# Decayed cumulative sum after a matmul: own gate tiles for the warm-up, the decay squares written by ScalarE, and a new order for the first 32 slots

## The chip, the core and the metric

The kernel runs on one NeuronCore of a Trainium2 chip. The core has five engines that run their own instruction queues in order: TensorE (PE; its weight loads are listed apart as PEld), VectorE (DVE), ScalarE (ACT), GpSimd (POOL) and SyncE (SP, which only issues DMAs here). The metric is the device time of one execution in microseconds (us). Before the change the median of four runs is 908.17 us.

## The reference, cut to what matters

```python
B, S, D = 16, 2048, 1024
# x: (B, S, D) f32, w: (D, D) f32, decay: (D,) f32 in 0.05 .. 0.95
xw = x @ w
out[:, 0, :] = xw[:, 0, :]
for t in range(1, S):
    out[:, t, :] = decay[None, :] * out[:, t - 1, :] + xw[:, t, :]
```

For each batch and each output column the product `x @ w` runs through a first-order recurrence along time, with one decay per column.

## The kernel before

**Tiling.** The 16 x 2048 rows are cut into 64 chunks of 512 time steps (`TL`), four for each batch. Two neighbouring chunks form a group. One group and one set `n` of 128 output columns (there are K = 8) form a *slot*, which is one tile of 128 columns by 1024 time steps; only the last group has one chunk. A slot needs 16 matmuls: 8 blocks of the contraction (k) for each of the two chunks, each 128x128 weights against 128x512 of x, summed in PSUM.

**Input.** POOL loads x as bf16 into `xb` (`load`, line 101; 3 buffers), a quarter (32 partitions) per DMA. VectorE turns it in 32x32 blocks into `xw` (`turn`, line 110; 2 buffers), two bf16 at a time, and a copy takes the even and odd rows apart into `xt` (`part`, line 119; 5 buffers), which is what TensorE reads. Part m of `xt` serves k = 2m and 2m + 1. The weights come in by DMA in four pieces (halves of the columns h, even or odd rows e) and are copied to `wsb` (`settle`, line 295); sixteen such copies are numbered 0 to 15, by h, e and m.

**The recurrence** has two ways. An unpaired tile is scanned by VectorE straight from PSUM (`scan`, L216, over 1024 steps). A paired tile is first folded: ScalarE copies PSUM to `xs` (`copy`, L178) and scales the odd columns by the decay (`odd`, L164), POOL adds the two (`join`, L191), VectorE scans half the steps with the squared decay (L196), then ScalarE scales the result (`even`, L164) and POOL fills in the other half (`fill`, L241). Pairing takes work from VectorE and gives it to ScalarE and POOL. Each fourth tile is unpaired, and the slots named in `flips` are the other way round. `save` keeps the last column for the next group of the same batch (L245); `zero` writes the column before the first step (POOL memset, or ScalarE copy of the kept column, L187).

**Output.** VectorE turns the scanned tile back (`back`, L253); after four tiles SP stores them in four DMAs (L274).

**The order of the work** is written out by hand. All instructions are pinned to the order in which the program emits them, so each engine works through its own part of that order. At each slot the matmuls are emitted, then the deeds that `agenda` lists for that slot; from slot 34 on a rule (`usual`) makes the list, and the last 20 slots have their own. A deed is a letter and a number:

- M, U: loads of halves of chunks 0 and 1, of weight pieces; L: the next x load of a list
- W, w: one weight copy, by VectorE or by ScalarE
- K: a warm-up copy and its spins; D: the decay and its squares; d: the squares once more, into PSUM (`square_again`, line 350)
- E, F, G: quarter turns of chunks 0 and 1, and their copies by VectorE (F) and ScalarE (G)
- T: a whole turn of a chunk; t, u: its first and second half; X, Y: the copies of its two halves by ScalarE
- p, g, z, j: copy, odd, zero, join; S: scan; h, c, k: even, fill, save; B: back

**The start.** While the first loads are under way, TensorE multiplies zeros (`spin`, line 309) so that its clock is up when data comes: 22 matmuls, then for each quarter q of chunk 0 a copy of one column of x into `idle` (`spin_on`, line 327) and three more matmuls that read `idle`. Slots 0 to 3 are computed together at slot 0, in the order in which pieces of chunks 0 and 1 come in: 32 matmuls of 256 columns (even k of chunk 0), 16 of 512 (odd k), then 64 of 256 (chunk 1). They go to three PSUM buffers `ps` and, for tile 3, to `spare` and `spare1`. Slots 4 to 7 take even k first. Slots 8 and 9 are computed together: chunk 2 for both, then chunk 3 for both. Slot s from 4 on takes one of the three `ps` buffers in turn, and waits until the tile before in it has been read.

Of the kernel before, what the change touches and what calls it, by code (L numbers as in the profile page):

```python
# [10 lines left out]
BF16 = mybir.dt.bfloat16  # L11
# [3 lines left out]
def _ap(ap_obj: bass.AP, new_ap, extra_offset=0):  # L15
    return dataclasses.replace(
        ap_obj,
        ap=[list(p) for p in new_ap],
        offset=ap_obj.offset + extra_offset,
    )  # L20
# [5 lines left out]
def kernel(  # L26
# [26 lines left out]
    nc = tc.nc  # L53
    pin = tc.keep_in_program_order
    B, S, D = x.shape
    assert w.shape == (D, D)

    NQ = 4
    P = 32
    CQ = D // NQ  # L60
    K = CQ // P
    M = K // 2
    TL = 512
    NJ = TL // P
# [5 lines left out]
    const = ctx.enter_context(tc.tile_pool(name="const", bufs=1))  # L70
# [5 lines left out]
    def ring(pool, name, count, shape, dtype=FP32):  # L76
        i = turns[name] = turns.get(name, -1) + 1
        return pool.tile(shape, dtype, name=f"{name}{i % count}")

    def quad(q):  # L80
        return slice(q * P, (q + 1) * P)
# [8 lines left out]
    squares = [const.tile([128, K], FP32, name="squares")]  # L90
# [6 lines left out]
    xb_of = {}  # L97
# [12 lines left out]
    def turn(c, j0=0, j1=NJ, m0=0, m1=M):  # L110
        if c not in xw_of:
            xw_of[c] = ring(sb, "xw", 2, [128, M, NJ, P, 2], BF16)
        src = xb_of[c][:, j0:j1].rearrange("p j c -> p (j c)").bitcast(FP32)
        dst = xw_of[c].rearrange("p m j i e -> p (m j i e)").bitcast(FP32)
        pin(nc.vector.transpose(  # L115
            out=dst.rearrange("p (m j i) -> p j m i", m=M, i=P)[:, j0:j1, m0:m1],
            in_=src.rearrange("p (j m c) -> p j m c", m=M, c=P)[:, :, m0:m1]))

    def part(c, copy, m0, m1, j0=0, j1=NJ):
        if c not in xt_of:  # L120
            xt_of[c] = ring(sb, "xt", 5, [128, M, 2, TL], BF16)
        src = xw_of[c][:, m0:m1, j0:j1].rearrange("p m j i e -> p m e (j i)")
        pin(copy(out=xt_of[c][:, m0:m1, :, j0 * P:j1 * P], in_=src))  # L123
# [176 lines left out]
    idle = const.tile([128, TL], BF16, name="idle")  # L300
    spare = ring(psp, "spare", 1, [128, TL])
# [4 lines left out]
    pin(nc.vector.memset(rows, 0.0))  # L306
    pin(nc.scalar.copy(out=touch, in_=idle[:, 0:1]))

    def spin(count):
        for _ in range(count):  # L310
            pin(nc.tensor.matmul(  # L311
                out=spare, lhsT=idle[:, 0:128], rhs=idle, start=True, stop=True))

    spin(22)
    H = NJ // 2
    halves = ((0, H), (H, NJ))
    for q in range(NQ):
        pin(nc.sync.dma_start(
            out=rows[q * P:q * P + R],
            in_=_ap(decay, [[P, R], [CH, 2], [1, P]], q * CR)))  # L320
# [4 lines left out]
            load(i // 2, q, *halves[i % 2])  # L325

    def spin_on(q):
        pin(nc.scalar.copy(out=idle[quad(q), 0:1], in_=xb_of[0][quad(q), 0, 0:1]))  # L328
        spin(3)

    def load_part(i):
        load_w((nc.gpsimd,), *((0, 1), (1, 0), (1, 1))[i])
# [13 lines left out]
    def square(i):  # L346
        pin(nc.vector.tensor_tensor(
            out=squares[-1][:, 0:K], in0=dec, in1=dec, op=ALU.mult))

    def square_again(i):  # L350
        squares.append(ring(psp, "spare1", 1, [128, TL]))
        square(0)


    ident = const.tile([128, 128], FP32, name="ident")
# [37 lines left out]
    slots += [([c], n) for c in groups[-1] for n in range(K)]  # L393
    tiles = []

    def turn_half(half):
        def act(c):
            if half == 0:
                turn(c, 0, NJ, 0, 2)
            else:  # L400
                turn_and_load(c, 2)
        return act

    def turn_and_load(c, m0=0):
        turn(c, 0, NJ, m0, M)
        if 2 <= c < nch - 3:
            loads.extend((c + 3, q) for q in range(NQ))

# [4 lines left out]
        "C": lambda s: tiles[s % len(slots)].complete(),  # L413
        "B": lambda s: tiles[s % len(slots)].back(),
        "T": turn_and_load,
        "t": turn_half(0),
        "u": turn_half(1),
        "X": lambda c: part(c, nc.scalar.copy, 0, 2),
        "Y": lambda c: part(c, nc.scalar.copy, 2, M),
        "x": lambda c: part(c, nc.vector.tensor_copy, 0, 2),  # L420
# [6 lines left out]
        "F": lambda i: part_one(i, nc.vector.tensor_copy),  # L427
        "G": lambda i: part_one(i, nc.scalar.copy),
        "K": spin_on,
        "D": decays,  # L430
        "d": square_again,
        "I": identity,
        "V": ending,
# [9 lines left out]
        "L": lambda i: load(*loads.pop(0)) if loads else None,  # L443
    }
    agenda = {
        -99: "M0 M1 U0 M2 M3 U1 U2 D W0 w1 W2 w3 K0 K1 K2 K3 E0 F0 G1 E1 F2 G3 E2 F4 G5 E3 F6 G7 W4 w5 W6 w7 E4 F8 G9 E5 F10 G11 E6 F12 G13 E7 F14 G15 L L L",
        0: "W8 w10 W9 W11",
        1: "S0 L",
        2: "L p1 z1",
        3: "L p2 z2 L B0 g1 L w15 W12 j1 S3 k0 w14 w13 L g2",  # L450
        4: "L d k3 j2 B3 p4 S1 L g4 z4 L",
        5: "t2 h1 j4 k1 S2 X2 c1 S4 k2 h2",
        6: "B1 k4 h4 c2 p5 u2 c4 g5 t3 p6 j5 B4",
        7: "g6 Y2 L u3 L z5 j6 B2 X3 S5 L z6 L Y3 S6 L L S7 k6 k5 L h5 h6 c5 T4",
        8: "p8",
        9: "c6 k7 g8",
        10: "p9 L g9 B7 j8 X4 B6 L j9",
        11: "B5 z8 p10 L g10 S8 z9 z10 j10 z11 Y4 S9",
        12: "L S10 h8 h9 c8 T5 h10 c9 p11 B8",
        13: "g11 c10 p12 B9 X5 L L B10 j11 Y5",  # L460
        14: "T6 L z12 g12 j12 S13 z14 X6",
        15: "L p14 S11 L g14 B13 h11 j14 Y6",
        16: "S12 c11 S14 h12 L p15 B11 c12 g15",
        17: "T7 L z15 p16 j15 g16 h14 L S15 X7 c14 B12",
        18: "j16 h15 B14 p17 L g17 z16 z17 c15 S16 Y7",
        19: "j17 B15 h16 L S17 k16 p18 z18 L T8 c16 h17",
        20: "k17 g18 c17 p19 B16 X8 j18 B17 L",
        21: "g19 S18 L Y8 z19 j19 S20 L h18 k18 c18",
        22: "p21 S19 z21 k20 g21 L T9 h19 j21 k19 c19",
        23: "B20 p22 L g22 B18 j22 B19 z22 L",  # L470
        24: "S21 p23 z23 X9 S22 h21",
        25: "k21 S24 g23 c21 k22 Y9 j23 B21 h22",
        26: "c22 S23 z25 p25 g25 B24 h23 j25 B22 k23 c23",
        27: "T10 z26 p26 g26 j26 B23 X10 S25",
        28: "Y10 S27 z28 h25 S26 c25",
        29: "p28 B27 g28 h26 j28 B25 c26 S28 z29",
        30: "p29 T11 g29 h28 j29 B26 c28",
        31: "p30 S29 z30 g30 B28 j30 h29 c29 S30",
        32: "S31 B29 h30 c30 p32 g32 z32 j32 B30 B31 L L",
        33: "p33 g33 z33 j33 S32 h32 c32 k32 L L",  # L480
        -20: "z-20",
# [17 lines left out]
        -2: "S-3 S-4",  # L499
        -1: "S-2 h-4 c-4 a-1 b-1 V",  # L500
    }
    flips = (0, 11, 13, 15, 19, 20, 23, 24, -19, -18, -16, -11, -8, -6, -3, -2)
    later = {}
    begun = {"T": 12, "X": 11, "Y": 11}
    for c in range(5, nch):
# [127 lines left out]
```

## Time and profile before

| What | Value |
|---|---|
| median of 4 runs | 908.17 us (908.13 to 908.73) |
| profiled execution | 908.43 us, span 906.6 us |
| granted TensorE clock | 0.999 of full speed |
| busy share: TensorE, VectorE, ScalarE, POOL | 99%, 91%, 76%, 73% |
| VectorE busy from 32 to 62 us | 100% |
| ScalarE busy from 42 to 52 us | 10.0 of 10 us |
| VectorE's waits on x, whole run | 6.1 us in 5 waits, longest 2.5 |
| DMA traffic | 204.77 MB, mean 226 GB/s |

A timeline row gives the start, the busy time, the engine, the line, the operation, its output and inputs, shapes, and a count; in brackets stands how long the engine was idle before it and what ended that wait. A row of the waits gives who waited for whom, then the total in us, the number of waits and the longest. Matmuls overlap by their pipeline, so their pace is read from start to start.

### The profile page before, as it was taken

To read this page: it belongs to the slowest core of one execution; us is meant where nothing else is said; L and a number is where in the kernel's file an instruction comes from. 1 tells how busy PE (TensorE), PEld (TensorE's weight loads), DVE (VectorE), ACT (ScalarE), POOL (GpSimd) and SP (SyncE) were. 2 spreads that over 40 slices of the span, in tenths; PEclk is the share of its full clock that TensorE was granted. 3 is DMA by queue.
4 is the path that set the end of the run, shared out by engine and by line. 5 is a ranking of instruction groups with operands and counts; after the bars stand their busy time and mean duration, and the time that the engine had idled before them with its cause. 6 is when DMAs were issued, how large, how long until landed. Compare 5 with 4: busy or idle time off the path is not lost.

```text
span 906.6 us, 11980 instructions
## 1 busy us (share of the span) xinstructions
PE 893.3 (99%) x4120; PEld 411.4 (45%) x4202; DVE 827.9 (91%) x622; ACT 684.9 (76%) x950; POOL 657.8 (73%) x756
## 2 busy tenths in 40 slices
PE   8999999999999999999999999999999999999997
PEld 4444444444444444444444444444444444444444
DVE  4989998999999999999999999999999999999997
ACT  4799867877877778778778778777787787787742
POOL 7888768778777777777677786777777776776622
PEclk9999999999999999999999999999999999999999
DMA  9999999999999999999999999999999999999868
GB/s 193 166 211 215 217 253 213 215 235 252 255 252 239 248 251 246 251 242 230 223 235 226 224 231 224 236 229 224 232 232 225 228 233 222 227 231 213 176 146 233
DMA packets 402542, 204.77 MB, mean 226 GB/s; under 512 B 8752, under 2 KB 401456, under 8 KB 402480
## 3 DMA queue, kind: packets, MB, share of 16 engines
q1 hardware_dynamic: 265168, 134.76, 60.9%
q0 software_dynamic: 137024, 68.70, 56.5%
q8 instruction: 33, 0.54, 0.2%
q10 hardware_dynamic: 288, 0.52, 0.2%
q14 instruction: 29, 0.24, 0.1%
HBM read 138.42 MB, written 134.22 MB: 301 GB/s over the span
## 4 chain that ended last, share of the span: by engine, by line
PE 95%; ACT 2%; DVE 2%; issue 1%; POOL 0%; DVEq 0%; ACTq 0%
PE ps L126 92%; PE spare L311 1%; DVE so L216 1%; PE spare L126 1%; ACT xs L178 1%; ACT h L164 1%; ACT xt L123 0%; DVE ot L253 0%; DVE so L196 0%; ACT wsb L297 0%; POOL xs L191 0%; PE spare L375 0%; PE ps L375 0%; ACT idle L328 0%; ACT keep L245 0%
## 5 line engine op out<-in xcount | busy, mean ns | idle before, releaser
L126 PE MATMUL ps<-xt,wsb 128*128 128x512 bf16 (+1 forms) x4010 | 873.6, 377 | 6.0 <-ACT xt L123 1.4
L126 PEld LDWEIGHTS <-wsb 128*128 128x128 bf16 x4152 | 406.1, 98 | 480.5 <-issue 2.1
L191 POOL TENSOR_TENSOR xs<-h,xs 128x512 f32<-128x512 f32 (+1 forms) x190 | 243.3, 1281 | 193.9 <-ACT h L164 94.0
L178 ACT COPY xs<-ps 128x1024 f32<-128x1024 f32 (+1 forms) x190 | 189.8, 999 | 156.8 <-PE ps L126 146.2
L253 DVE STREAM_TRANSPOSE ot<-so 128x1024 f32<-128x1024 f32 (+1 forms) x260 | 300.1, 1191 | 1.3 <-POOL so L241 0.4
L241 POOL TENSOR_TENSOR so<-h,xs 128x512 f32<-128x512 f32 (+1 forms) x190 | 241.9, 1274 | 41.0 <-ACT h L164 20.3
L123 ACT COPY xt<-xw 128x2048 bf16<-128x2048 bf16 (+1 forms) x132 | 240.3, 1825 | 7.4 <-DVE xw L115 7.3
L105 POOL DMA_DIRECT2D xb<-in_x_dram x264 | 173.9, 660 | 2.7 <-DMA ot<-in_w_dram 1.3
L164 ACT ACTIVATE h<-so,dec 128x512 f32<-128x512 f32 (+1 forms) x190 | 145.2, 766 | 23.8 <-DVE so L196 20.3
L115 DVE STREAM_TRANSPOSE xw<-xb 128x2048 f32<-128x2048 f32 (+2 forms) x72 | 147.5, 2050 | 6.1 <-DMA xb<-in_x_dram 6.1
L196 DVE TENSOR_TENSOR_SCAN so<-spare,keep,xs 128x512 f32<-128x512 f32 (+1 forms) x96 | 119.3, 1245 | 27.6 <-POOL xs L191 27.3
L196 DVE TENSOR_TENSOR_SCAN so<-spare,xs 128x512 f32<-128x512 f32 x94 | 114.4, 1219 | 28.5 <-POOL xs L191 25.8
L164 ACT ACTIVATE h<-ps,dec 128x512 f32<-128x512 f32 (+1 forms) x190 | 130.5, 687 | 0.0
L216 DVE TENSOR_TENSOR_SCAN so<-dec,keep,ps 128x1024 f32<-128x1024 f32 (+1 forms) x36 | 77.1, 2143 | 0.1
L216 DVE TENSOR_TENSOR_SCAN so<-dec,ps 128x1024 f32<-128x1024 f32 x33 | 74.6, 2261 | 1.8 <-PE ps L126 1.2
L245 ACT COPY keep<-so 128x1 f32<-128x1 f32 x136 | 25.5, 188 | 12.8 <-DVE so L216 12.8
L187 ACT COPY so<-keep 128x1 f32<-128x1 f32 x96 | 18.2, 192 | 5.2 <-DVE ot L253 5.2
L311 PE MATMUL spare<-idle 128*128 128x512 bf16 x34 | 10.8, 474 | 2.4 <-DVE idle L305 1.2
L126 PE MATMUL spare<-xt,wsb 128*128 128x256 bf16 (+1 forms) x60 | 12.6, 322 | 0.0
L185 POOL MEMSET so<- 128x1 f32 x94 | 10.9, 116 | 0.6 <-DVE ot L253 0.6
L290 POOL DMA_DIRECT2D ot<-in_w_dram x12 | 6.7, 560 | 3.2 <-DMA xb<-in_x_dram 1.9
L311 PEld LDWEIGHTS <-idle 128*128 128x128 bf16 x34 | 3.6, 117 | 9.2 <-issue 3.5
(32 smaller groups left out, 30.5 us busy)
## 6 DMA issues: line engine op xcount, KB each, us to landing
out_dram<-ot SPq DMA_DIRECT2D x248, 512.0 KB, 10.9
xb<-in_x_dram POOLq DMA_DIRECT2D x248, 256.0 KB, 7.9
out_dram<-ot SPq DMA_DIRECT2D x12, 256.0 KB, 4.3
xb<-in_x_dram POOLq DMA_DIRECT2D x16, 128.0 KB, 5.7
ot<-in_w_dram POOLq DMA_DIRECT2D x12, 128.0 KB, 5.1
out_dram<-xb SPq DMA_DIRECT2D x3, 256.0 KB
ot<-in_w_dram ACTq DMA_DIRECT2D x2, 256.0 KB, 5.1
ot<-in_w_dram SPq DMA_DIRECT2D x2, 256.0 KB, 4.7
```

Of the source, the lines that this page charges most:

```text
L105: pin(nc.gpsimd.dma_start(out=xb_of[c][quad(q), j0:j1], in_=_ap(x, [[D, P], [P * D, j1 - j0], [1, CQ]], (b * S + t0 + j0 * P) * D + q * CQ)))
L115: pin(nc.vector.transpose(out=dst.rearrange("p (m j i) -> p j m i", m=M, i=P)[:, j0:j1, m0:m1], in_=src.rearrange("p (j m c) -> p j m c", ...
L123: pin(copy(out=xt_of[c][:, m0:m1, :, j0 * P:j1 * P], in_=src))
L126: pin(nc.tensor.matmul(out=ps[:, t0:t1] if ps.shape[1] >= t1 else ps, lhsT=wsb[:, k, n].rearrange("p q i -> p (q i)"), rhs=xt[:, k // 2, k ...
L164: pin(nc.scalar.activation(out=h, in_=src, func=mybir.ActivationFunctionType.Copy, scale=dec[:, self.n:self.n + 1]))
L178: pin(nc.scalar.copy(out=self.xs, in_=self.ps))
L191: pin(nc.gpsimd.tensor_tensor(out=odds, in0=self.g, in1=odds, op=ALU.add))
L196: pin(nc.vector.tensor_tensor_scan(out=so[:, 3:T + 2:2], data0=squares[-1][:, n:n + 1].to_broadcast([128, T // 2]), data1=self.xs[:, 1:T:2 ...
L216: pin(nc.vector.tensor_tensor_scan(out=so[:, t + 2:t + 2 + size], data0=dec[:, n:n + 1].to_broadcast([128, size]), data1=ps, initial=befor ...
L241: pin(nc.gpsimd.tensor_tensor(out=self.so[:, 2:T + 2:2], in0=self.h, in1=self.xs[:, 0:T:2], op=ALU.add))
L245: pin(nc.scalar.copy(out=self.keep, in_=self.so[:, self.T + 1:self.T + 2]))
L253: pin(nc.vector.transpose(out=outlet.ot[:, :, c0:c0 + P], in_=self.so[:, 2 + t0:2 + t0 + nj * P].rearrange("p (i t) -> p i t", t=P)))
```

## The change

Four things change. (1) Each of the four warm-up groups has its own 128x128 tile `gate`, zeroed by VectorE before the first spin; the copy from x goes to that tile, and the group's spins use it as weights. The last group spins twice instead of three times. (2) The second squaring into PSUM (`d`) is a ScalarE copy of the squares made before, where it was a VectorE multiplication. (3) The agenda of the head and of slots 0 to 31 is reordered, D comes after G3 instead of before W0, and which engine does some weight copies changes. In `flips`, 1 and 12 come in and 13 and 15 go: tiles 1, 12 and 15 become unpaired, tile 13 paired. (4) Chunks 2 and 3 are turned whole (T) instead of in halves (t, u).

```diff
+    gates = [const.tile([128, 128], BF16, name=f"gate{q}") for q in range(NQ)]
+    for gate in gates:
+        pin(nc.vector.memset(gate, 0.0))
+
+    def spin(count, by):
         for _ in range(count):
-            pin(nc.tensor.matmul(
-                out=spare, lhsT=idle[:, 0:128], rhs=idle, start=True, stop=True))
-    spin(22)
+            pin(nc.tensor.matmul(out=spare, lhsT=by, rhs=idle, start=True, stop=True))
+    spin(22, idle[:, 0:128])
...
     def spin_on(q):
-        pin(nc.scalar.copy(out=idle[quad(q), 0:1], in_=xb_of[0][quad(q), 0, 0:1]))
-        spin(3)
+        pin(nc.scalar.copy(out=gates[q][quad(q), 0:1], in_=xb_of[0][quad(q), 0, 0:1]))
+        spin(3 if q < NQ - 1 else 2, gates[q])
...
     def square_again(i):
         squares.append(ring(psp, "spare1", 1, [128, TL]))
-        square(0)
+        pin(nc.scalar.copy(out=squares[1][:, 0:K], in_=squares[0]))
...
-        -99: "M0 M1 U0 M2 M3 U1 U2 D W0 w1 W2 w3 K0 K1 K2 K3 E0 F0 G1 E1 F2 G3 E2 F4 G5 E3 F6 G7 W4 w5 W6 w7 E4 F8 G9 E5 F10 G11 E6 F12 G13 E7 F14 G15 L L L",
-        0: "W8 w10 W9 W11",
+        -99: "M0 M1 U0 M2 M3 U1 U2 W0 w1 W2 w3 K0 K1 K2 K3 E0 F0 G1 E1 F2 G3 D E2 F4 G5 E3 F6 G7 W4 w5 W6 w7 E4 F8 G9 E5 F10 G11 E6 F12 G13 E7 F14 G15 L L L",
+        0: "W8 w11 W9 W10",
         1: "S0 L",
-        2: "L p1 z1",
-        3: "L p2 z2 L B0 g1 L w15 W12 j1 S3 k0 w14 w13 L g2",
-        4: "L d k3 j2 B3 p4 S1 L g4 z4 L",
-        5: "t2 h1 j4 k1 S2 X2 c1 S4 k2 h2",
-        6: "B1 k4 h4 c2 p5 u2 c4 g5 t3 p6 j5 B4",
-        7: "g6 Y2 L u3 L z5 j6 B2 X3 S5 L z6 L Y3 S6 L L S7 k6 k5 L h5 h6 c5 T4",
+        2: "L",
+        3: "L p2 L S1 g2 z2 L w14 j2 w12 w13 S3 k0 L w15",
+        4: "k1 L",
+        5: "p4 B0 L d g4 S2 z4 k3 j4 T2 h2 L",
+        6: "k2 p5 c2 g5 S4 L X2 j5 B1",
+        7: "Y2 L B2 L L T3 p6 z5 z6 g6 k4 h4 j6 B3 X3 L S5 L Y3 S6 L L S7 c4 h6 k6 h5 c6 B4",
         8: "p8",
-        9: "c6 k7 g8",
-        10: "p9 L g9 B7 j8 X4 B6 L j9",
-        11: "B5 z8 p10 L g10 S8 z9 z10 j10 z11 Y4 S9",
-        12: "L S10 h8 h9 c8 T5 h10 c9 p11 B8",
+        9: "c5 g8 B7",
+        10: "k7 k5 z8 j8 p9 B5 g9 S8 j9 z9 T4",
+        11: "h8 p10 c8 g10 S9 X4 L j10 B8",
+        12: "p11 L B6 L Y4 T5 L z10 z11",
+        13: "g11 h9 j11 S10 X5 S12 L c9 Y5",
+        14: "L S11 h10 B9 h11 c10 p13 T6",
+        15: "c11 g13 z13 p14 j13 B10 g14 X6 j14 B11",
+        16: "L S13 z14 Y6 L L S15 h13 L c13",
...
-    flips = (0, 11, 13, 15, 19, 20, 23, 24, -19, -18, -16, -11, -8, -6, -3, -2)
+    flips = (0, 1, 11, 12, 19, 20, 23, 24, -19, -18, -16, -11, -8, -6, -3, -2)
```

Slots 17 to 31 are reordered in the same way; the two functions that turned half a chunk go.

## The prediction

> **What bounds the kernel now.** I read four views: the shares by engine, the list of TensorE's waits, TensorE's timeline over the first 48 us, and ScalarE's and VectorE's timelines beside it.
>
> ```profile
> PE 893.3 (99%) x4120; PEld 411.4 (45%) x4202; DVE 827.9 (91%) x622; ACT 684.9 (76%) x950; POOL 657.8 (73%) x756
> PE 95%; ACT 2%; DVE 2%; issue 1%; POOL 0%; DVEq 0%; ACTq 0%
> PE ps L126 <- ACT xt L123: 1.4, 1, 1.4
> PE spare L311 <- DVE idle L305: 1.2, 1, 1.2
> PE spare L311 <- ACT idle L328: 1.2, 4, 0.3
> PE ps L126 <- ACT wsb L297: 0.3, 1, 0.3
> ```
>
> TensorE (PE) is busy 99% and carries 95% of the chain that ended last. The four rows below are all its waits in the run. Asked from 60 us on, the view has none, and every 128x512 matmul follows its predecessor by 0.216 us. So from about 48 us TensorE runs at its own pace, and a change to the first 32 slots moves the end by as much as it moves TensorE's arrival at that steady run.
>
> ```profile
> 9.08 0.82 PE L311 MATMUL spare<-idle 128*128 128x512 bf16 x3 [0.33 <-ACT idle L328]
> 12.40 0.82 PE L311 MATMUL spare<-idle 128*128 128x512 bf16 x3 [0.28 <-ACT idle L328]
> 13.05 0.49 PE L126 MATMUL ps<-xt,wsb 128*128 128x256 bf16 x3
> 26.99 2.32 PE L126 MATMUL ps<-xt,wsb 128*128 128x512 bf16 x9
> 29.64 12.69 PE L126 MATMUL ps<-xt,wsb 128*128 128x512 bf16 x57 [0.34 <-ACT wsb L297]
> 43.71 4.62 PE L126 MATMUL ps<-xt,wsb 128*128 128x512 bf16 x20 [1.38 <-ACT xt L123]
> ```
>
> Real matmuls start at 13.05. From start to start (0.216 is due) the wait at 29.64 costs 0.50 us, the one at 43.71 1.54, and a last one at 47.31, on the next xt copy, 0.15.
>
> ```profile
> 9.84 0.71 DVE L115 STREAM_TRANSPOSE xw<-xb 128x512 f32<-128x512 f32 x1
> 12.15 0.19 ACT L328 COPY idle<-xb 32x1 bf16<-32x1 bf16 x1 [0.91 <-PE spare L311]
> 12.32 0.71 DVE L115 STREAM_TRANSPOSE xw<-xb 128x512 f32<-128x512 f32 x1 [0.21 <-DMA xb<-in_x_dram]
> 12.37 2.40 ACT L123 COPY xt<-xw 128x512 bf16<-128x512 bf16 x4
> ```
>
> The first turn is done at 10.55, but ScalarE is held by the fourth warm-up copy until 12.35: each copy into the shared `idle` waits 0.91 for the spins that read it.
>
> **The head, part by part.** With a tile per group no copy waits for spins. The copies follow their landings (the quarters of the first half land at 7.65, 8.40, 8.94, 9.72), the last at 9.78-9.97. 22+11 spins instead of 34, two after the last gate, end near 10.45. The next limit is data. The first turn starts at 9.84 as before, since the last quarter lands at 9.72 (a turn starts 0.12 after its landing at 17.25 and 19.98). F0 ends at 11.02, so the first real matmul stands at 11.07 instead of 13.05.
>
> That is not the gain, because the second half of chunk 0 lands at 12.20. D (0.66 us from 8.41 to 9.07) moves from before W0 to between F2, which frees VectorE at 12.01, and E2: E2 starts at 12.67, not 12.32. Then F4 ends at 13.85, E3 at 14.47, F6 at 14.93. TensorE waits until 13.90, takes two lots of four (0.44 each), waits to 14.98 and ends its 32 half-length matmuls at 15.85; before they ended at 13.05 + 32 x 0.109 = 16.54. **Head: -0.70.** All up to 26.29 (was 26.99) follows undelayed: the chunk 1 copies end at 18.74, 19.82 and 22.55, and are needed at 19.31, 21.06 and 23.5. If D still stood first, it would be -1.05.
>
> The four gate memsets (about 0.1 each, after `rows`, 0.11 for 64 f32) run while POOL issues its first x load, 1.31-2.04. No row shows a memset over a POOL issue. The nearest is the issue at 9.22 beside VectorE's casts: 0.73 against 0.54. The bounds are 0 and 0.4 us (all four memsets) on every landing. I take 0, since the x packets run back to back once started and the queue is eight deep. W0 and W2, now at 7.2, meet the issue at 7.93 instead, the same 0.2.
> The Trainium skill (SBUF — State Buffer, Who interferes with whom) says that VectorE copies and casts in a two-port mode lock GpSimd's descriptor writes out, while on trn2 a memset does not. The 0.73 agrees; by the rule the memsets cost 0.
>
> **Step 4** needs S0 (23.73 + 2.29 = 26.02, TensorE at 26.29) and the weights W12-W15, which are now four ScalarE copies in the order 14, 12, 13, 15 behind p2 and g2. Tile 2 ends at 25.44. ScalarE's steps from its rows: p 0.91, g 0.59, w 0.52, with a w 0.63 long. So w12 ends at 28.13 and w13 at 28.65; TensorE wants them at 28.02 and 28.61 and waits 0.14 + 0.09. **0.50 becomes 0.23: -0.27**, and step 4 ends at 29.98 (before 30.94).
>
> **Step 8** is the largest term. VectorE goes in order without a hole from S0: S0 2.22, S1 (tile 1 is now unpaired, a scan of 1024) 2.20, S3 2.55, B0 1.13, so S2 starts at 31.83 and ends at 33.02; T2 from 32.96 to 35.2, S4, B1, B2 1.12 each, T3 from 38.53 to 40.8. T2 and T3 whole cost 2.2 each where two halves cost 1.13 + 1.13. Chunks 2 and 3 land at 31.5 and 37.1: covered. Then ScalarE, full from h2 at 33.04: h2 0.67, k2 0.1, p5 0.91, g5 0.59, X2 1.8, Y2 1.8, p6 0.91, g6 0.59, k4 0.1, h4 0.67, X3 1.8, Y3 1.9 long, which sums to 11.84 and ends at 44.88. TensorE begins step 8 at 29.98 + 3 x 3.46 = 40.36 and wants Y2 (there at 39.0) at 41.2, X3 (43.1) at 43.8 and Y3 at 44.69. It goes on at 44.90, after 0.21. Before, the same matmul began at 47.31. **1.69 becomes 0.21: -1.48.** What paid: tile 1 unpaired takes a copy, two scalings and a bit (some 2.3 us) off ScalarE ahead of Y3, and Y2 no longer stands behind the second turn.
>
> The squares. VectorE wrote them to PSUM in 1.21 (30.86), where the same operation into SBUF took 0.17 at 8.90; on ScalarE no row writes PSUM. Bounds: 0.1 (step of its 128x1 copies) and 1.12 (VectorE's). I take 0.1, the same engine's row. It stands behind p4 (30.05-30.95) and after S3 has read that buffer (30.7), and S2 waits for it. At 1.12 S2 and everything to Y3 would come 0.3 later. ScalarE idles from 31.9 to 33.0, which covers the rest.
> The Trainium skill (SBUF — State Buffer, Who interferes with whom) also says that a two-input VectorE operation shuts GpSimd's reads out and is shut out by them, and ScalarE never; POOL's join ran 30.72-32.02, which fits the 1.21. By the rule ScalarE's copy costs its 0.1-0.2, by the VectorE row 1.1.
>
> **Later slots.** POOL's joins and loads in the new order: c4 45.7, c6 47.0, c5 48.3; p9 waits for c5 to free its buffer, till 48.35, and is needed only by step 12 at 54.4. S7 frees step 10's buffer at 46.3; TensorE wants it at 47.5. T4 moves from 48.8 to 50.9; X4 and Y4 are done by 57.6, needed at 68.3. SP's first stores follow B3, at 41.9 instead of 44.5, and share the DMA engines with the loads. The chunk 5 and 6 loads are issued at 35-39 and 42-44 instead of 42-45 and 46-51. VectorE's sum to slot 32 grows by two scans (2 x 1.05) and shrinks by the squares (1.12) and a W (0.25): +0.7 us; it idled 3.6 us between 60 and 110. **0.**
>
> **Sum:** 0.70 + 0.27 + 1.48 = 2.45, say 2.4. The profiled execution took 908.43 (span 906.6 and 1.8 around it): 906.0. The median shown is 0.26 below it: **905.8**.
>
> **Rivals.** A difference under 0.2% (1.8 us) can't be told from none here.
> 1. *ScalarE comes late at Y3.* Twelve operations stand in one row with 0.2 us missing already; 1 us more there (squares at 1.12, a late S2, the memsets' 0.4) is 1 us lost. For it: ScalarE is full from 42 to 52 before. Against it: its hole at 31.9. Time: 906.3 to 907.5.
> 2. *The head gives nothing*, because data and not spins bound it, with D in VectorE's way: the 0.70 is lost, 906.5.
> 3. *Slower: VectorE falls behind.* It is full from 24 to 63 already, and two more tiles are scanned whole. T6 stands before S13 and S15, and S15 must free step 18's buffer at 75.2; by my sum it ends at 71.9, if chunk 6 lands before 64 (65.97 before). From a landing at 67.5 each us is lost on TensorE, from 71.7 the kernel is slower; at 74: 905.8 + 6.5 = 912. Against it: those loads are issued 4 to 6 us earlier.
> 4. *All waits vanish*: D costs nothing and steps 4 and 8 run through: 1.05 + 0.50 + 1.69 = 3.2, 904.9.
>
> **Numbers.** Forecast (with 4) 0.68, rivals 1 and 2 together 0.22, rival 3 0.10. Range 904.9 (rival 4) to 908.2, which takes in rivals 1 and 2 and leaves out most of 3. Faster 0.68, same 0.22, slower 0.10.
>
> **What would show it.** The head: first real matmul near 11.1, with waits on the chunk 0 copies, the first 32 done by 15.9. Step 4: two waits on `wsb` below 0.2. Step 8: one short wait on `xt` near 44.9, none on chunk 2. The squares: a ScalarE row of 0.2. Later: no TensorE wait. The forecast is wrong if TensorE shows a wait after 48 us, or if its matmuls step by more than 0.216.

## The result, and the profile after

The changed kernel takes 906.87 us (median of 29 runs, 906.21 to 908.13) against 908.34 us (47 runs) for the kernel before: a ratio of 0.9983, 95% interval 0.9978 to 0.9989. That is 1.5 us less, where 2.4 were forecast. In a later set it took 906.38 against 908.61 (ratio 0.9976, 0.9968 to 0.9985): 2.2 us less. The profiled execution took 907.26 us with a span of 905.4, so it is one of the slower of its kind (the second longest of 29).

The page of the changed kernel, shares by engine and the waits of TensorE over the whole run (who waited for whom, total us, times, longest):

```profile
PE 892.1 (99%) x4119; PEld 411.2 (45%) x4201; DVE 828.5 (92%) x622; ACT 681.2 (75%) x945; POOL 652.7 (72%) x751
PE 94%; DVE 2%; issue 1%; ACT 1%; DMA 1%; POOL 0%; DVEq 0%; ACTq 0%; POOLq 0%
PE spare L315 <- DVE idle L305: 1.2, 1, 1.2
PE ps L126 <- DVE xt L123: 1.0, 2, 0.9
PE spare L315 <- ACT gate L331: 1.0, 1, 1.0
PE ps L126 <- DVE so L216: 0.2, 1, 0.2
```

The four short waits of the spins and the long one on `xt`, which ended at 43.71, are gone. One wait of 1.0 stands where the four were: for the first gate copy, which ScalarE makes behind its weight copies. New are a wait on VectorE's copies of chunk 0 (the head is now bound by data and by VectorE's work on it), DMA in the chain that ended last, and a wait on a scan (`so`, L216) that the kernel before does not have. TensorE's timeline, changed kernel:

```profile
8.63 2.55 PE L315 MATMUL spare<-idle,gate 128*128 128x512 bf16 x11 [1.01 <-ACT gate L331]
11.36 0.49 PE L126 MATMUL ps<-xt,wsb 128*128 128x256 bf16 x3 [0.18 <-DVE xt L123]
14.38 0.49 PE L126 MATMUL ps<-xt,wsb 128*128 128x256 bf16 x3 [0.86 <-DVE xt L123]
26.82 23.34 PE L126 MATMUL ps<-xt,wsb 128*128 128x512 bf16 x102
...
873.74 1.89 PE L126 MATMUL ps<-xt,wsb 128*128 128x512 bf16 x8 [0.17 <-DVE so L216]
```

The eleven gate spins run in one piece, real matmuls start 1.7 us earlier, and from 26.82 on there is no gap worth a line until 873.74. To see what became of each microsecond I compare the start of the same matmul (by its place in the order of TensorE's records) in two executions. The table gives TensorE's lead over the profiled kernel before, in us: at the first matmul after the 32 half-length ones of chunk 0, inside slot 4, in the steady run from 200 us on, and at the last matmul of line 126; beside them stands when the two halves of chunk 0 landed, and the median. Each row is one profiled execution.

| kernel | first half lands | second half lands | lead, chunk 0 | slot 4 | steady | last | median us |
|---|---|---|---|---|---|---|---|
| before | 9.72 | 12.20 | - | - | - | - | 908.34 |
| changed | 10.01 | 12.56 | 0.16 | 0.29 | 1.90 | 1.57 | 906.87 |
| changed, again (after_again) | 9.31 | 11.95 | 0.86 | 0.99 | 2.60 | 2.26 | 906.38 |
| gates_only | 9.82 | 12.23 | 0.90 | -0.46 | -0.22 | -0.22 | 908.41 |
| plan_only | 9.60 | 12.29 | -0.07 | 0.06 | 1.65 | 1.65 | 906.80 |
| gates_w12 | 9.56 | 12.24 | 1.01 | 0.92 | 2.26 | 2.26 | 906.92 |
| d_late | 9.20 | 11.80 | 1.45 | 1.58 | 3.18 | 2.85 | 906.34 |
| tile1_paired | 9.84 | 12.36 | 0.41 | 0.50 | 1.00 | 0.67 | 907.60 |
| squares_dve | 10.02 | 12.62 | 0.24 | 0.37 | 1.60 | 1.27 | 906.99 |
| gates_scalar | 9.75 | 12.40 | 0.41 | 0.54 | 2.14 | 2.14 | 906.22 |
| best1 | 9.73 | 12.20 | 0.64 | 0.90 | 2.43 | 2.43 | 905.41 |
| best1_again | 9.38 | 12.11 | 1.13 | 1.52 | 3.16 | 3.16 | 905.30 |

Two things stand out in the rows of the changed kernel. Its lead depends on the landing of x: between its own two executions the first half lands 0.70 us apart and the second 0.61, and the lead at the end of chunk 0 differs by 0.70. And 0.33 us of the lead is lost at 873 us both times.

### The profile page after: what moved, and what is told of

Read it like the earlier page. It is cut to its first block, busy times and chain, and to the rows that moved or that the text cites. A ratio compares the mean times of both kernels' runs of the same rounds, so it can differ in the third digit from the quotient of the medians.

```text
span 905.4 us, 11969 instructions
## 1 busy us (share of the span) xinstructions
PE 892.1 (99%) x4119; PEld 411.2 (45%) x4201; DVE 828.5 (92%) x622; ACT 681.2 (75%) x945; POOL 652.7 (72%) x751
## 4 chain that ended last, share of the span: by engine, by line
PE 94%; DVE 2%; issue 1%; ACT 1%; DMA 1%; POOL 0%; DVEq 0%; ACTq 0%; POOLq 0%
PE ps L126 93%; DVE so L216 1%; DMA xb<-in_x_dram 1%; PE spare L126 1%; ACT h L164 0%; DVE xw L115 0%; ACT xs L178 0%; DVE ot L253 0%; DVE so L196 0%; POOL xb L105 0%; ACT xt L123 0%; DVE xt L123 0%; POOL xs L191 0%; PE spare L378 0%; ACT wsb L297 0%
## 5 line engine op out<-in xcount | busy, mean ns | idle before, releaser
L191 POOL TENSOR_TENSOR xs<-h,xs 128x512 f32<-128x512 f32 (+1 forms) x188 | 240.7, 1280 | 199.0 <-ACT h L164 93.3
L178 ACT COPY xs<-ps 128x1024 f32<-128x1024 f32 (+1 forms) x188 | 187.7, 998 | 162.1 <-PE ps L126 151.7
L241 POOL TENSOR_TENSOR so<-h,xs 128x512 f32<-128x512 f32 (+1 forms) x188 | 239.4, 1275 | 36.8 <-ACT h L164 23.2
L115 DVE STREAM_TRANSPOSE xw<-xb 128x2048 f32<-128x2048 f32 (+1 forms) x70 | 147.3, 2105 | 4.9 <-DMA xb<-in_x_dram 4.9
L216 DVE TENSOR_TENSOR_SCAN so<-dec,keep,ps 128x1024 f32<-128x1024 f32 (+1 forms) x37 | 79.5, 2149 | 0.1
L216 DVE TENSOR_TENSOR_SCAN so<-dec,ps 128x1024 f32<-128x1024 f32 x34 | 76.8, 2262 | 1.5 <-ACT h L164 1.0
L315 PE MATMUL spare<-idle 128*128 128x512 bf16 x22 | 6.4, 462 | 1.2 <-DVE idle L305 1.2
```

The costliest lines, as they stand in the source:

```text
L115: pin(nc.vector.transpose(out=dst.rearrange("p (m j i) -> p j m i", m=M, i=P)[:, j0:j1, m0:m1], in_=src.rearrange("p (j m c) -> p j m c", ...
L178: pin(nc.scalar.copy(out=self.xs, in_=self.ps))
L191: pin(nc.gpsimd.tensor_tensor(out=odds, in0=self.g, in1=odds, op=ALU.add))
L216: pin(nc.vector.tensor_tensor_scan(out=so[:, t + 2:t + 2 + size], data0=dec[:, n:n + 1].to_broadcast([128, size]), data1=ps, initial=befor ...
L241: pin(nc.gpsimd.tensor_tensor(out=self.so[:, 2:T + 2:2], in0=self.h, in1=self.xs[:, 0:T:2], op=ALU.add))
```

## The experiments

There were ten runs, of eight new kernels, and of the changed kernel and best1 once more. They came in three sets, each on another chip; each set shares its runs of the kernel before.

**gates_only.** The kernel before with the gate tiles alone.

```diff
-        pin(nc.scalar.copy(out=idle[quad(q), 0:1], in_=xb_of[0][quad(q), 0, 0:1]))
-        spin(3)
+        pin(nc.scalar.copy(out=gates[q][quad(q), 0:1], in_=xb_of[0][quad(q), 0, 0:1]))
+        spin(3 if q < NQ - 1 else 2, gates[q])
```

> The kernel before with the gate tiles (and 2 spins after the last gate) as its only change; agenda, flips, squares and turns as before. Theory A (the head is worth something, D in VectorE's way took most of it back in the changed kernel): D stands first here, so the second half of chunk 0 is turned at its landing plus 0.12 us and the 32 half-length matmuls of chunk 0 end 0.6 to 1.0 us earlier than the 16.54 of before; everything behind is paced by TensorE and follows, so the time falls by 0.6 to 1.0 us (ratio 0.9989 to 0.9993). Theory B (x's landing bounds the head whatever the spins do): the 32 end within 0.3 us of 16.54 and the ratio is 0.9997 to 1.000.

908.41 against 908.42, ratio 0.9999 (0.9991 to 1.0008). Neither theory fits: the head did give 0.90 us, as A has it, and the time did not move, as B has it. VectorE's timeline and then POOL's, of gates_only, show why:

```profile
26.07 1.25 DVE L253 STREAM_TRANSPOSE ot<-so 128x1024 f32<-128x1024 f32 x1
27.24 2.37 DVE L297 COPY wsb<-ot 128x512 bf16<-128x512 bf16 x1
29.54 1.21 DVE L216 TENSOR_TENSOR_SCAN so<-dec,spare 128x512 f32<-128x512 f32 x1
```

```profile
26.79 1.27 POOL L105 DMA_DIRECT2D xb<-in_x_dram  x2
28.16 1.29 POOL L191 TENSOR_TENSOR xs<-h,xs 128x512 f32<-128x512 f32 x1
```

W12 is one weight copy of 128x512. In the kernel before it took 0.25 us, beside a join of POOL (VectorE's row, then POOL's):

```profile
28.06 0.25 DVE L297 COPY wsb<-ot 128x512 bf16<-128x512 bf16 x1
28.04 1.42 POOL L191 TENSOR_TENSOR xs<-h,xs 128x512 f32<-128x512 f32 x1 [0.44 <-ACT h L164]
```

In gates_only it starts 0.8 us earlier, at 27.24, while POOL is issuing loads, and ends 0.16 us after POOL's join does, at 29.61. TensorE waits for it, 1.69 us in its own timeline:

```profile
29.67 13.12 PE L126 MATMUL ps<-xt,wsb 128*128 128x512 bf16 x59 [1.69 <-DVE wsb L297]
```

The Trainium skill (SBUF — State Buffer, Who interferes with whom) says that a VectorE copy in a two-port mode and any GpSimd operation exclude each other for a whole instruction, and that whoever comes first keeps the ports. For the join the rows agree: the copy, which found POOL at work, ends just behind it. In the kernel before the two began within 0.02 us of each other, too close to say which was first, and it was the join that grew, to 1.42 from 1.30. For the load issues they don't agree as plainly. The copy waited through two issues and the join, and not for one instruction. And most weight copies that start inside a load issue are not held: in the kernel before two run within the issue from 22.86 to 23.65 in 0.29 us each, and it is the issue that is long, 0.79 for 0.64. What held W12 from 27.24 to the start of the join at 28.16 is not shown.

**gates_w12.** The same kernel with W12 and W13 on ScalarE, which the skill's section exempts.

```diff
-        3: "L p2 z2 L B0 g1 L w15 W12 j1 S3 k0 w14 w13 L g2",
+        3: "L p2 z2 L B0 g1 L w12 w13 j1 S3 k0 w15 w14 L g2",
```

> The kernel with the gate tiles alone (ratio 0.9999; its weight copy W12 took 2.37 us on VectorE at 27.24 instead of 0.25, while POOL issued a load and ran a join), with W12 and W13 given to ScalarE ahead of w15. Theory A (that stretched copy ate the head's 0.9 us): the copy is gone, TensorE's wait at step 4 is under 0.4 us, its lead of 0.6 to 0.9 us from the head stays up to step 8, and the time falls by 0.6 to 1.2 us: ratio 0.9987 to 0.9993. Theory B (the head's lead is lost anyway, to loads that land when they land): the wait only moves, to step 8 or to another weight copy, and the ratio is 0.9997 to 1.0003.

906.92 against 908.37, ratio 0.9989 (0.9980 to 0.9998; its runs spread from 906.35 to 909.82, so the interval is wide). Theory A: the head's 1.01 us is still 0.92 in slot 4. The wait at step 4 itself is 0.58 from start to start, more than the 0.4 expected and no shorter than the 0.50 before. The lead then grows to 2.26, more than expected, at step 8, where the wait is 0.26 and 0.15 and was 1.54 and 0.15. VectorE's timelines say where that comes from: the turn t2, from whose end ScalarE works without a hole to the copies that step 8 needs, starts at 32.05 instead of 34.25. Of these 2.20 us S0 brings 0.96, since TensorE is ahead, W12 off VectorE some 0.2, and the squares some 1.0: they fall on no join here and take 0.17 us instead of 1.21. So two edits to the old order reach what the whole new order reaches, and nearly half of it is a row that happened to miss a join.

**plan_only.** The changed kernel without the gates.

```diff
-        pin(nc.scalar.copy(out=gates[q][quad(q), 0:1], in_=xb_of[0][quad(q), 0, 0:1]))
-        spin(3 if q < NQ - 1 else 2, gates[q])
+        pin(nc.scalar.copy(out=idle[quad(q), 0:1], in_=xb_of[0][quad(q), 0, 0:1]))
+        spin(3)
```

> The changed kernel without the gate tiles (warm-up copies into idle, 34 spins as before). Theory A (nearly all of the gain is the new order of slots 4 to 9): real matmuls start at 13.05, the waits at step 4 and step 8 are 0.3 to 0.5 and under 0.3 us, and the time falls by 1.2 to 1.7 us (ratio 0.9981 to 0.9987), within 0.3 us of the whole change. Theory B (the two halves need each other: with a later start the new order has its waits elsewhere): the time falls by less than 0.7 us.

906.80 against 908.42, ratio 0.9979 (0.9970 to 0.9988). Theory A. The first matmul stands at 13.12, the waits of step 4 are 0.28 and 0.08, that of step 8 is 0.15, and the lead of 1.65 is kept to the end. By the medians the gates of the changed kernel thus add nothing (906.87 against 906.80, in different sets). By the traces they bring the head 0.2 to 0.9 us, and the changed kernel loses 0.33 in the tail, which plan_only does not (see gates_scalar).

**d_late.** D moved to where VectorE idles.

```diff
-        -99: "... F2 G3 D E2 F4 G5 E3 F6 G7 W4 w5 W6 w7 E4 ...",
+        -99: "... F2 G3 E2 F4 G5 E3 F6 G7 W4 w5 W6 w7 D E4 ...",
```

> The changed kernel with the decay and its squares (D, 0.76 us on VectorE) moved from between F2 and E2 to behind w7, where VectorE idles for 1.7 us. Theory A (D costs the head its gain): E2 starts at the landing of the second half plus 0.12 instead of 0.56 after it, the 32 half-length matmuls end 0.4 us earlier than in the changed kernel, and the time is 0.4 us below it: 906.3 to 906.6 against 908.34 (ratio 0.9976 to 0.9981). Theory B (what is won in the head is lost again at step 8, which waits for ScalarE anyway): head 0.4 earlier, wait at step 8 0.4 longer, ratio 0.9983 as the changed kernel.

906.34 against 908.42, ratio 0.9975 (0.9965 to 0.9984). The medians alone don't settle it, the trace does. VectorE in the changed kernel, then in d_late:

```profile
11.96 0.47 DVE L123 COPY xt<-xw 128x512 bf16<-128x512 bf16 x1
12.36 0.23 DVE L344 STREAM_TRANSPOSE cols<-rows 128x64 f32<-128x64 f32 x1
12.62 0.29 DVE L345 COPY dec<-cols 128x8 f32<-128x8 f32 x1
12.94 0.17 DVE L350 TENSOR_TENSOR squares<-dec 128x8 f32<-128x8 f32 x1
13.12 0.71 DVE L115 STREAM_TRANSPOSE xw<-xb 128x512 f32<-128x512 f32 x1
```

```profile
11.15 0.45 DVE L123 COPY xt<-xw 128x512 bf16<-128x512 bf16 x1
11.92 0.71 DVE L115 STREAM_TRANSPOSE xw<-xb 128x512 f32<-128x512 f32 x1 [0.32 <-DMA xb<-in_x_dram]
```

The turn E2 (the last row of each) starts 0.56 after the landing at 12.56 with D in its way, and 0.12 after the landing at 11.80 without. So D costs 0.44. Of the 1.29 us by which d_late leads the changed kernel at the end of chunk 0, some 0.8 are its earlier landings. Step 8 gave nothing back.

**tile1_paired.** Tile 1 paired again, its ScalarE and POOL work where ScalarE has holes.

```diff
-        2: "L",
-        3: "L p2 L S1 g2 z2 L w14 j2 w12 w13 S3 k0 L w15",
-        4: "k1 L",
-        5: "p4 B0 L d g4 S2 z4 k3 j4 T2 h2 L",
+        2: "L p1 z1",
+        3: "L p2 L g1 z2 L w14 j1 w12 w13 S3 k0 L w15 g2",
+        4: "j2 L",
+        5: "p4 B0 L d g4 S1 S2 h1 c1 k1 z4 k3 j4 T2 h2 L",
-    flips = (0, 1, 11, 12, ...
+    flips = (0, 11, 12, ...
```

> The changed kernel with tile 1 paired again (its copy, two scalings, join and fill back on ScalarE and POOL, placed where ScalarE had holes; its scan half as long). Theory A (tile 1 unpaired pays for step 8): h2, p5 and with them Y3 come 0.6 to 1.2 us later, TensorE waits 0.6 to 1.3 us at step 8 and the time is 0.5 to 1.0 us above the changed kernel: ratio 0.9988 to 0.9994. Theory B (the order, not the pairing, pays): Y3 within 0.3 us of its place, ratio 0.998 to 0.9986.

907.60 against 908.42, ratio 0.9990 (0.9981 to 0.9999). Theory A. TensorE's timeline of tile1_paired has the wait at step 8 again:

```profile
28.62 16.97 PE L126 MATMUL ps<-xt,wsb 128*128 128x512 bf16 x75 [0.16 <-ACT wsb L297]
46.37 3.83 PE L126 MATMUL ps<-xt,wsb 128*128 128x512 bf16 x17 [0.78 <-ACT xt L123]
```

From start to start the two waits there are 0.31 and 0.94 us, where the changed kernel has 0.14 in all: 1.1 us of the 1.6 us that the changed kernel gains from slot 4 to the steady run. With the pairing the edit also moves S1 and g2 to later places; another order with tile 1 paired was not tried.

**squares_dve.** The squares into PSUM by VectorE again.

```diff
-        pin(nc.scalar.copy(out=squares[1][:, 0:K], in_=squares[0]))
+        square(0)
```

> The changed kernel with the second squaring back on VectorE (a multiplication into PSUM). Theory A (1.21 us before was the join that POOL ran at that time): here POOL has no join at that place, the row lasts about 0.2 us, S2 starts within 0.2 us of its place and the time is that of the changed kernel, 906.9. Theory B (VectorE's write to PSUM costs 1.2 us in itself): S2, h2 and Y3 come 1.0 us later and the time is 907.3 to 907.9.

906.99 against 908.37, ratio 0.9983 (0.9974 to 0.9993). Theory A for the row; the kernel before (VectorE's row and POOL's join beside it), then squares_dve with the S2 that follows, then S2 in the changed kernel:

```profile
30.86 1.21 DVE L347 TENSOR_TENSOR spare<-dec 128x8 f32<-128x8 f32 x1
30.72 1.30 POOL L191 TENSOR_TENSOR xs<-h,xs 128x512 f32<-128x512 f32 x1
```

```profile
32.44 0.15 DVE L350 TENSOR_TENSOR spare<-dec 128x8 f32<-128x8 f32 x1
32.69 1.22 DVE L196 TENSOR_TENSOR_SCAN so<-spare,xs 128x512 f32<-128x512 f32 x1
```

```profile
32.43 1.19 DVE L196 TENSOR_TENSOR_SCAN so<-spare,xs 128x512 f32<-128x512 f32 x1
```

The same instruction took 1.21 at 30.86 in the kernel before, from 0.14 after a join of POOL began to its end, and takes 0.15 here, 0.25 before the next join, and 0.17 in gates_only and gates_w12. It never was the write to PSUM. But the row is not free in the new order either. VectorE has no hole before S2, so S2 starts 0.26 later, X3 and Y3 on ScalarE start 0.29 later, and TensorE's list of waits in squares_dve has one that the changed kernel's has not:

```profile
PE ps L126 <- ACT xt L123: 0.4, 1, 0.4
```

From start to start it waits 0.52 at step 8, where the changed kernel waits 0.14, and its steady lead stays 0.37 short of what its lead in slot 4 promised. About 0.1 of that is a later landing of chunk 1, which held S0; the other quarter of a microsecond is the squares.

**gates_scalar.** Zeroing the gates on ScalarE, so that VectorE's code is four instructions shorter.

```diff
-        pin(nc.vector.memset(gate, 0.0))
+        pin(nc.scalar.copy(out=gate, in_=idle[:, 0:128]))
```

> The changed kernel with the four gates zeroed by ScalarE (copies of zeros from idle, in its idle time before 7 us) instead of by VectorE; VectorE has four instructions fewer. Theory A (the 0.36 us stall of VectorE at the scan at 863.67 comes from where its code stands, since it shows in the three kernels with 1150 VectorE rows and in neither of those with 1146 and 1149): the scan starts 0.08 us after TensorE is done, TensorE shows no wait near 873 and the end keeps 0.33 us more of the lead. Theory B (it comes from TensorE's earlier arrival): the wait of 0.33 near 873 stays. The time alone would tell them apart badly: 906.5 against 906.9.

906.22 against 908.37, ratio 0.9977 (0.9969 to 0.9986). Theory A. VectorE around the scan of the tail, in the kernel before, the changed kernel and gates_scalar:

```profile
865.20 2.29 DVE L216 TENSOR_TENSOR_SCAN so<-dec,ps 128x1024 f32<-128x1024 f32 x1 [0.61 <-ACT h L164]
```

```profile
863.67 2.29 DVE L216 TENSOR_TENSOR_SCAN so<-dec,ps 128x1024 f32<-128x1024 f32 x1 [0.99 <-ACT h L164]
```

```profile
863.06 2.29 DVE L216 TENSOR_TENSOR_SCAN so<-dec,ps 128x1024 f32<-128x1024 f32 x1 [0.62 <-ACT h L164]
```

The scan waits for TensorE to finish its tile, which it does 0.08 before the scan starts in the first and the third kernel, and 0.45 before in the second; the releaser that the rows name had been done for 0.47 and 0.84 us. VectorE has 1145, 1150 and 1146 rows in these three, its sequencer's included. All five runs with 1150 (changed twice, d_late, tile1_paired, squares_dve) show the 0.98 or 0.99 before the scan and TensorE's wait of 0.33 near 873; all others, 1145 to 1149, show 0.61 or 0.62 and none. Counted up to the scan, the five have 1087 rows of VectorE before it, and the others 1082 to 1086. The lead is not what decides: at that time it is 1.00 to 3.18 us in the five, and 2.14 to 3.16 in four of the others.

**best1, best1_again and after_again.** What the runs so far point to: the gates by ScalarE, D behind w7, the weight copies of step 4 in the order in which TensorE reads them, and h4 behind Y3.

```diff
-        3: "L p2 L S1 g2 z2 L w14 j2 w12 w13 S3 k0 L w15",
+        3: "L p2 L S1 g2 z2 L w12 j2 w13 w14 S3 k0 L w15",
-        7: "... z5 z6 g6 k4 h4 j6 B3 X3 L S5 L Y3 S6 ...",
+        7: "... z5 z6 g6 j6 B3 X3 L S5 L Y3 k4 h4 S6 ...",
```

> The changed kernel with D behind w7, the gates zeroed by ScalarE, the weight copies of step 4 in the order 12, 13, 14, 15, and the scaling h4 with its k4 put behind Y3. Theory A (each of these waits is TensorE's own and they add up): against the changed kernel 0.45 from D, 0.3 at step 4 with 0.1 at step 8, 0.33 in the tail: 905.7 to 906.1, ratio 0.9969 to 0.9975. Theory B (they hide one another; the run that moves D alone already has what there is): 906.3, ratio 0.9975 to 0.998.

> The changed kernel as it is, to stand beside best1_again on one chip. If 0.9983 was its level: 0.998 to 0.9987, TensorE 1.6 to 2.4 us ahead of the kernel before from 60 us on (as the first x landings fall), and the wait of 0.33 at the scan of the tail again, since it hangs on the place of VectorE's code and not on chance.

> The kernel of best1 once more, beside the changed kernel on one chip. Theory A (waits add up): 0.9 to 1.3 us below the changed kernel, ratio to before 0.9967 to 0.9975, no wait of TensorE between 30 us and the last tile. Theory B (best1's 905.41 was a lucky chip): within 0.5 us of the changed kernel.

best1: 905.41, ratio 0.9970 (0.9959 to 0.9981), a little under the 905.7 to 906.1 expected. after_again came out better than expected, at a ratio of 0.9976 and with a steady lead of 2.60 for at most 2.4, and the wait of 0.33 in the tail came again. In the last set best1_again took 905.30 (905.23 to 905.67), ratio 0.9966 (0.9953 to 0.9978), beside 906.38 (906.13 to 906.66) for the changed kernel: 1.1 us below it, and 3.3 below the kernel before. The waits add up. TensorE in best1_again, from the middle of the head on:

```profile
13.46 0.49 PE L126 MATMUL ps<-xt,wsb 128*128 128x256 bf16 x3 [0.57 <-DVE xt L123]
25.85 36.43 PE L126 MATMUL ps<-xt,wsb 128*128 128x512 bf16 x163
```

What is left is the wait for the second half of chunk 0, and two delays of 0.11 and 0.10 us at steps 4 and 8. In the profile of best1 a weight load landed late as well (15.43 against 14.3 to 15.0 elsewhere but in squares_dve), which cost it 0.4 us; why it did was not looked into.

## Why the prediction was right, point by point

The time, 906.87, lies in the range, which is wide: it takes in all but a slowdown. 1.5 us (in the later set 2.2) stand against 2.4. Of the sum, 0.70 + 0.27 + 1.48, the first profile shows 0.16 + 0.14 + 1.55 and the second 0.86 for the head; the tail and the end took some of it back. The forecast of "faster by over 0.2%" was met in the later set and missed by a little in the first.

*Steady run.* That the end moves with TensorE's arrival holds: from 200 us to 857 us the lead of the changed kernel is 1.90 throughout, and 2.60 in its second execution; 2.45 was the sum.

*Head, 0.70.* The mechanism was right, down to D in VectorE's way, and the size was off in the first profile: 0.16, then 0.86 in the second. In the first, E2 started at 13.12 where 12.67 was worked out: 0.29 from the landing of the first half (10.01, not 9.72), 0.10 from D (0.76, not 0.66), the rest from F2. The 0.54 us that the head lacks are the largest term of the gap in the first profile. The landing was taken as a constant from one execution. It is none: over the eleven profiles of the kernels tried and of the change, the first half lands between 9.20 and 10.02 and the second between 11.80 and 12.62. With D where the change has it the head follows the first half, through VectorE's unbroken row from E0 to E2; with D moved behind w7 it follows the second.

*Gate memsets, 0 taken.* The first x load is issued in 0.73 us with them and without, and the kernels with memsets by VectorE have both the earliest landing (11.80) and the latest (12.62).

*Step 4, 0.27.* The waits are 0.28 and 0.08, for 0.14 and 0.09: 0.14 gained. The reading that was off is the end of tiles 0 and 2. S0 was put at 23.73 and tile 2 at 25.44, where TensorE's lead of 0.70 gives 23.87 for S0 (24.57 before). In the changed kernel p2, ScalarE's copy of tile 2, starts 0.67 before slot 4, where tile 2 was to end 0.85 before it; from there to the end of w12 it took what was worked out (2.63 for 2.69). What the prediction did not see is what that edit protects from. On VectorE the copy W12 would have taken the head's gain, as gates_only shows.

*Step 8, 1.48.* The wait is 0.14, for 0.21: 1.55 gained. ScalarE's row of twelve, from h2 to Y3, took 11.77 for 11.84. That tile 1 unpaired pays for it is shown: without it 1.1 us come back.

*Squares.* 0.18 on ScalarE, as taken. The bound of 1.12 from VectorE's row was no property of the write; in the new order VectorE's row is as short. What the edit is worth is the place in VectorE's full row, about a quarter of a microsecond at step 8 (squares_dve), which the sum did not name: it feared a cost on ScalarE, and the gain lay on VectorE.

*Later slots, 0.* This is the term whose mechanism was wrong, and by the prediction's own sign (a wait of TensorE after 48 us) this part of it failed. No wait comes up to 873 us, so rival 3 is out, but in the tail 0.33 us go at a scan that VectorE starts late, and the sum had TensorE's arrival carried to the end unchanged. Another 0.37 us of the gap in the first profile goes after the last matmul: the last store takes 3.17 us from issue to completion against 2.90, and 0.10 more pass from there to the end. The time from TensorE's last row to the end lies between 4.88 and 5.38 over all profiles, without a pattern.

*Rivals.* 1 did not come: measured from TensorE's arrival, Y3 was no later than worked out. 2 came for three quarters in the first profile (0.16 of the 0.70 was left), through the landing and D, and not in the second.

## What to carry to other kernels

A gain at the head of a chain reaches the end only if no later step is fixed by something else; try the edit alone, and if it gives nothing, look for the row whose duration changed. A short VectorE copy on the critical path can grow tenfold when it meets POOL's work (2.37 us for 0.25 here, though most copies beside a load issue did not): give it to ScalarE, or place it where POOL waits. When the first work of a kernel is bound by a DMA's landing, one profile gives one draw of it, so take two or three before a few tenths are put down to an edit.

## What the runs showed of the hardware that was not expected

- A VectorE copy of 128x512 bf16 took 2.37 us beside POOL's load issue and join, where 0.25 to 0.30 is its usual time. Beside a load issue alone most kept that time, and a few took 0.32 to 0.52, one of them in the changed kernel (0.52 at 23.36).
- A scan late in the program starts 0.37 us late in the five runs whose VectorE program has 1150 rows, and in none with 1145 to 1149. The four memsets of the gates at the start move that scan along VectorE's code, and giving them to ScalarE ends the delay. That a fetch of code stands behind it was not shown: an 8 KB instruction transfer starts 3.0 us after that scan's start in all five, but one also does in the others, 3.3 us after it in gates_only and 6.0 in the rest.
- The landing of the first x loads differs by 0.8 us between executions, on several chips, of programs whose first loads are the same, and it passes on to the end. How much is the chip and how much the execution was not taken apart.
